# A streaming-encoder trunk: the first norm's factors spread over the partitions by TensorE, and residual loads, additions and operand preparation moved in the down-projection

## The chip, the cores and the metric

The kernel runs on one core of one Trainium2 chip. The time is device microseconds of that core, the median of several runs. The profile is one execution of the program, taken by the hardware profiler; its times are microseconds from the start of its span.

## What is computed

Two layers on 1024 tokens of width 1024, float32. Layer 0 mixes tokens by differential attention, layer 1 by latent attention. Behind each stands a gated MLP with a causal convolution; its last step is the down-projection. Cut to what the change touches:

```python
def rms_norm(x, g):
    xf = x.astype(jnp.float32)
    y = xf * lax.rsqrt(jnp.mean(xf * xf, axis=-1, keepdims=True) + NORM_EPS)
    return (y * g.astype(jnp.float32)).astype(x.dtype)

h = rms_norm(x, attn_norm_g[i])          # g: one factor per feature
x = x + diff_attention(h, ...)           # layer 0; mla_attention in layer 1
h = rms_norm(x, ffn_norm_g[i])
x = x + (jax.nn.silu(g) * val) @ w_down  # conv_ffn: 2816 x 1024
...
return rms_norm(x, final_norm_g)
```

## The kernel before

Every large product is done in three: each operand is split into a high part, rounded to fp32r (`hi`, L127, on ScalarE as a rule), and a low part, the rest (`lo`, L130, on VectorE as a rule), and `mm3` (L119 to L121) sums high x low, high x high and low x high in PSUM. The core's memory is cut by hand into places: 14 of 8 KB per partition (`s0` to `s13`), 16 of 4 KB (`u`), 14 of 2 KB (`h`). PSUM has two double banks (`S`, from `big`) and four single ones: three with the tag `b`, one with the tag `u`. A tile that takes a bank waits until the last reader of the tile before it there is done.

In regions marked `manual_schedule`, the instructions of the engines named stand in the order in which the code issues them; elsewhere a scheduler with simulated times sets the order. Each engine works its queue strictly in that order, SP's queue (most DMA issues) too. A DMA issued from SP is held, besides its data, until the one eight places before it has landed.

*The prologue* (`diff_attention`, from L412). Token tiles of 128 x 1024 are loaded one by one. For each: `squares` (L157, ScalarE) sums the squares, `root` (L164 on VectorE, L167 on GpSimd) makes the reciprocal root, `norm` (L422, VectorE) multiplies the tile by the root and by the factors `g`, `turn` (L430) transposes it in eight 128x128 pieces into two `b` banks, `high` and `low` split it. `g` is the vector `attn_norm_g[0]`, loaded by `gain` (L193) as 128 copies of 4 KB: one DMA of 512 KB into `s11`, second in SP's queue. Between the tiles stand the splits of the first head's weights (`w_high`, `w_low`) and its first products on half a token block (`piece`, 24 matmuls of 128x256 each). The order is written out by hand for TensorE, VectorE and ScalarE.

*The down-projection* (`down`, L1261). The inner dimension of 22 blocks is taken in two parts. Blocks 0 and 1 are done plainly: for each of the eight token tiles, 12 matmuls of 128x512 into two banks, `y`, then two additions of `y` to the residual `X` (L1429, VectorE). The token tiles alternate between two `b` banks and a `b` and the `u` bank, so a tile waits for the additions two tiles before it. The other 20 blocks are done by a Strassen-like scheme on ten pairs of blocks: two groups of five pairs, each with seven products (M5, M1, M3, M2 and so on), each product over its five pairs j. One step is one product of one pair: 12 matmuls. A step's operands are sums of quarter blocks (`sums`, L1293, VectorE, where there are any), their high parts (`high`, ScalarE) and low parts (`low`, VectorE). `advance` issues them ahead of use: in one call the sums of two steps later, the high parts of the next step, and the low parts of the current one, all counted by `at.low`. It is called after the plain token tiles 4, 6 and 7, and after each step. The quarter blocks are loaded by `fetch` (L1283), the residual by `fetch_x` (L1339), 1 MB for two token tiles. Products are added to the residual by `evict` (L1449). While the plain tiles run, VectorE also finishes the up-projection's last block (L1113, L1119), whose result goes to DRAM (L1122, from ScalarE's queue) and comes back as a block of the fifth pair.

*Attention of layer 1* (`MlaStep`) is ordered by the scheduler: scores into `S` banks (L119 to L121), exponentials on ScalarE (L2013), transposes of the probabilities (L252), products with the values (L2033, L2034), and the next heads' projections (`b` banks).

## Time and profile before

| | us |
|---|---|
| median of 3 runs | 2403.01 (2402.82 to 2404.68) |
| the profiled execution | 2402.48 |
| its span | 2400.7 |
| busy: TensorE, VectorE, ScalarE, GpSimd | 2345.5, 1947.9, 1290.0, 612.4 |
| prologue and first projections, 0 to 45: TensorE busy | 33.1 |
| opening of the down-projection, layer 0, 990 to 1020 | 28.1 of 30 |
| the same, layer 1, 2189 to 2207 | 14.6 of 18 |
| last stretch of layer 0 and latent projections, 1300 to 1341 | 33.7 of 41 |

The rows of the timeline give start and length of an instruction (us), its engine, its line in the program, the operation with what it writes and reads, and in brackets how long the engine was idle before it and what released it. SPq and ACTq are the engines' instruction queues, where DMAs are issued. A matmul's length holds its way through the array; the pace is the distance from one start to the next.

### The profile page before, as it was taken

What the parts mean: (1) busy time and instruction counts of PE and PEld (TensorE: products, weight loads), DVE (VectorE), ACT (ScalarE), POOL (GpSimd) and SP (SyncE); (2) the same over time, 40 slices, a digit from 0 to 9 for tenths busy, and PEclk for the clock granted to TensorE, in tenths of its full rate; (3) what the DMA queues carried; (4) which work ended last, traced back from release to release, by engine and by line L of the source; (5) the groups of instructions that cost most, each with busy time, mean ns of one, the idle gap of its engine ahead of it and who ended that gap; (6) DMA issues with size and microseconds to landing.
All of it is one profiled execution on the core that took longest, in us unless ns stands there. A gap on an engine that the chain in (4) does not pass through costs nothing.

```text
span 2400.7 us, 32598 instructions
## 1 busy us (share of the span) xinstructions
PE 2345.5 (98%) x11936; PEld 1993.4 (83%) x11936; DVE 1947.9 (81%) x3180; ACT 1290.0 (54%) x2366; POOL 612.4 (26%) x484
## 2 busy tenths in 40 slices
PE   7999999999999999999999899999999999999998
PEld 7888888888888888788898789988888888887886
DVE  6888888858888888899864788886488888888997
ACT  5677777745444444444445777775354444443443
POOL 3555555424000000000132666664320000000001
PEclk9999999999999999999999999999999999999999
DMA  3011111333222222642221111123322222227502
GB/s 154 33 43 36 36 47 56 110 101 115 79 89 87 79 79 88 230 168 91 82 97 57 61 40 40 41 88 113 112 73 89 87 79 79 88 79 280 176 1 79
DMA packets 95792, 213.91 MB, mean 89 GB/s; under 512 B 8720, under 2 KB 33936, under 8 KB 95632
## 3 DMA queue, kind: packets, MB, share of 16 engines
q1 hardware_dynamic: 86448, 184.04, 23.1%
q10 hardware_dynamic: 9184, 27.79, 3.1%
q8 instruction: 94, 1.54, 0.3%
q14 instruction: 66, 0.54, 0.1%
HBM read 159.37 MB, written 52.43 MB: 88 GB/s over the span
## 4 chain that ended last, share of the span: by engine, by line
PE 85%; DVE 6%; DMA 3%; ACT 3%; POOL 2%; issue 2%; SPq 0%; POOLq 0%; DVEq 0%; ACTq 0%
PE S L119 13%; PE S L121 13%; PE S L120 13%; PE b L119 8%; PE b L120 8%; PE b L121 8%; PE u L119 4%; PE u L121 4%; PE u L120 4%; PE b L252 2%; PE u L2034 1%; PE u L2033 1%; PE S L1878 1%; PE S L1877 1%; DMA u<-g_d 1%
## 5 line engine op out<-in xcount | busy, mean ns | idle before, releaser
L167 POOL TENSOR_TENSOR st<-st,mhalf 128x1 f32<-128x1 f32 x56 | 36.1, 645 | 1312.7 <-DVE st L164 1304.9
L119 PE MATMUL S<-s,u 128*128 128x512 f32 (+1 forms) x800 | 302.1, 378 | 1.9 <-DVE s L130 1.9
L121 PE MATMUL S<-s,u 128*128 128x512 f32 (+1 forms) x800 | 301.2, 377 | 1.6 <-DVE u L130 0.8
L120 PE MATMUL S<-s,u 128*128 128x512 f32 (+1 forms) x800 | 301.0, 376 | 0.0
L127 ACT CAST u<-h 128x512 fp32r<-128x512 f32 (+2 forms) x242 | 145.5, 619 | 273.1 <-DVE h L1056 272.1
L119 PE MATMUL b<-s,u 128*128 128x512 f32 x588 | 230.7, 392 | 0.9 <-DVE u L130 0.4
L121 PE MATMUL b<-s,u 128*128 128x512 f32 x588 | 229.0, 390 | 0.0
L120 PE MATMUL b<-s,u 128*128 128x512 f32 x588 | 229.0, 389 | 0.0
L1113 DVE SCALAR_TENSOR_TENSOR u<-u,conv,u 128x1023 f32<-128x1023 f32 (+1 forms) x176 | 224.9, 1278 | 0.8 <-ACT u L1109 0.7
L149 POOL TENSOR_TENSOR u<-u,st 128x512 f32<-128x512 f32 (+7 forms) x160 | 172.1, 1085 | 171.5 <-DVE st L2019 104.7
L127 ACT CAST s<-u 128x512 fp32r<-128x512 f32 (+3 forms) x230 | 145.0, 665 | 99.2 <-PE u L121 35.4
L130 DVE TENSOR_TENSOR u<-b,u 128x512 fp32r<-128x512 f32 (+1 forms) x256 | 159.0, 632 | 21.6 <-ACT u L127 19.0
L119 PEld LDWEIGHTS S<-s,u 128*128 128x128 f32 x800 | 150.5, 188 | 30.2 <-DVE s L130 2.5
L121 PEld LDWEIGHTS S<-s,u 128*128 128x128 f32 x800 | 150.5, 188 | 29.5 <-DVE u L130 1.0
L120 PEld LDWEIGHTS S<-s,u 128*128 128x128 f32 x800 | 150.5, 188 | 27.3
L127 ACT CAST u<-b 128x512 fp32r<-128x512 f32 (+1 forms) x256 | 134.7, 546 | 69.2 <-PE b L1924 39.4
L119 PE MATMUL u<-s,s 128*128 128x512 f32 (+1 forms) x408 | 163.6, 401 | 1.9 <-DVE s L130 0.9
L121 PE MATMUL u<-s,s 128*128 128x512 f32 (+1 forms) x408 | 159.0, 390 | 0.0
L120 PE MATMUL u<-s,s 128*128 128x512 f32 (+1 forms) x408 | 158.8, 389 | 0.0
L1116 ACT ACTIVATE u<-u 128x1024 f32<-128x1024 f32 x44 | 46.7, 1062 | 187.4 <-DVE u L1113 187.4
L130 DVE TENSOR_TENSOR s<-u,s 128x512 fp32r<-128x512 f32 (+2 forms) x204 | 139.1, 714 | 9.2 <-ACT s L127 8.9
L130 DVE TENSOR_TENSOR u<-h,u 128x512 fp32r<-128x512 f32 x171 | 117.4, 687 | 32.6 <-ACT u L127 31.5
(280 smaller groups left out, 6527.0 us busy)
## 6 DMA issues: line engine op xcount, KB each, us to landing
u<-in_ffn_up SPq DMA_DIRECT2D x88, 512.0 KB, 3.9
g_d<-u ACTq DMA_DIRECT2D x44, 512.0 KB, 2.6
u<-in_ffn_down SPq DMA_DIRECT2D x66, 256.0 KB, 4.9
u<-g_d SPq DMA_DIRECT2D x62, 256.0 KB, 4.2
s<-in_da_wqkv SPq DMA_DIRECT2D x23, 512.0 KB, 3.6
x_d<-u SPq DMA_DIRECT2D x16, 512.0 KB, 2.9
s<-x_d SPq DMA_DIRECT2D x8, 1024.0 KB, 10.8
u<-o_d SPq DMA_DIRECT2D x24, 256.0 KB, 2.9
```

The source lines that it names most:

```text
L119: mm(out, lh, rl, start=first, stop=False, skip_group_check=onto)
L120: mm(out, lh, rh, start=False, stop=False, skip_group_check=onto)
L121: mm(out, ll, rh, start=False, stop=last, skip_group_check=onto)
L127: self.nc.scalar.copy(out, src)
L130: (eng or self.nc.vector).tensor_sub(out, src, hi.bitcast(F32))
L149: self.nc.gpsimd.tensor_mul(x, x, s.to_broadcast(list(x.shape)))
L167: nc.gpsimd.tensor_tensor(r, s, self.mhalf, ALU.pow)
L252: self.nc.tensor.transpose(ps[:, j * P : (j + 1) * P], probs[t][:, k : k + P], self.ident)
L1113: nc.vector.scalar_tensor_tensor(t[half][:, back:], u[half][:, : S - back], w, t[half][:, back:], ALU.mult, ALU.add)
L1116: nc.scalar.activation(t[0], t[0], AF.Silu)
L1877: nc.tensor.matmul(sc[c][:, b : b + m], ql[c][:, qs], kt[:, c, :m], start=True, stop=False)
L1878: nc.tensor.matmul(sc[c][:, b : b + m], qh[:, c, qs], kt[:, c, :m], start=False, stop=True)
```

## The change

In the prologue, the broadcast load of the factors is gone. The vector is loaded as 8 rows of 128 (4 KB, from ScalarE's queue, before its table load). TensorE transposes it into a column block of 128x8, VectorE copies that to SBUF, and eight transposes, each with one column broadcast over 128 columns as the operand, lay the factors out on all partitions in an `S` bank. The norms of tiles 0 and 1 read them there; ScalarE copies them to `s11` for tiles 2 to 7. Seven matmuls of 128x512 of ones into a `u` bank are added (`spin`), three behind the spread, two behind the transposes of tile 0 and two behind those of tile 1; their operand of ones is written by VectorE at the start. SP's queue is now in the order of the code in the prologue, as is GpSimd's, and the last part of the first value unit is inside the region.

In the down-projection, `advance` issues high, low, sums instead of sums, high, low; the last residual load is issued behind the four blocks of pair 3; and the additions of a token tile are issued in the code behind the next tile's matmuls.

```diff
+    def spin(self, n):
+
+        ps = self.bank("u")
+        for _ in range(n):
+            self.nc.tensor.matmul(ps, self.ones, self.wide, start=True, stop=True)
...
+        self.row = self.at("u13", [8, P])
+        nc.scalar.dma_start(self.row, a["attn_norm_g"][0:1, :].rearrange("o (k p) -> (o k) p", p=P))
         nc.scalar.preload_act_table_set("natural_log_exp_and_others")
...
+        self.wide = self.at("h4", [P, 512], F32R)
+        for j in range(4):
+            nc.vector.tensor_scalar(self.wide[:, j * P : (j + 1) * P], self.ident, 0.0, 1.0, ALU.mult, ALU.add)
...
+        queue = self.tc.manual_schedule(engines={mybir.EngineType.SP})
+        queue.__enter__()
...
-            nc.vector.scalar_tensor_tensor(x[i], x[i], r[i], g, ALU.mult, ALU.mult)
+            nc.vector.scalar_tensor_tensor(x[i], x[i], r[i], g[i], ALU.mult, ALU.mult)
...
         fetch_x(0)
-        g = self.gain("s11", a["attn_norm_g"][0])
         fetch_x(1)
...
+        column = self.bank()
+        nc.tensor.transpose(column[:, 0:KD], self.row, self.ident[0:KD, 0:KD])
+        gains = self.at("h5", [P, KD])
+        nc.vector.tensor_copy(gains, column[:, 0:KD])
+        spread = self.big()
+        for k in range(KD):
+            nc.tensor.transpose(spread[:, k * P : (k + 1) * P], gains[:, k : k + 1].to_broadcast([P, P]), self.ident)
+        g = [spread, spread] + 6 * [self.at("s11", [P, D])]
+        self.spin(3)
         squares(0)
         root(0)
         norm(0)
         squares(1)
+        nc.scalar.copy(g[2], spread)
         root(1)
         turns(0)
+        self.spin(2)
         high(0)
...
         turns(1)
+        self.spin(2)
         high(1)
...
         def advance(to, most=2):

             while at.low <= to and most:
-                sums(at.low + 2)
                 high(at.low + 1)
                 low(at.low)
+                sums(at.low + 2)
...
-        fetch_x(2)
-        for j, names in ((3, ("B12", "A21", "B11", "A22")), (4, ("B12", "A21", "B11", "A22")), (5, ("B12",))):
+        fetch_x(1)
+        for name in ("B12", "A21", "B11", "A22"):
+            fetch(3, name)
+        fetch_x(1)
+        for j, names in ((4, ("B12", "A21", "B11", "A22")), (5, ("B12",))):
...
+            if t:
+                taken(t - 1, *older)
+            older = y
...
-            for b in range(2):
-                x = X[t // 2][:, t % 2, b * 512 : b * 512 + 512]
-                nc.vector.tensor_add(x, x, y[b])
+        taken(NT - 1, *older)
```

What the change moves, first at the start of the program on TensorE. Before, its queue begins with the transposes of token tile 0 (`u_60_156`) and 1 (`u_62_160`) and the first product:

```order
L430 MATMUL b_186<-ident,u_60_156 128x128 x4
L430 MATMUL b_191<-ident,u_60_156 128x128 x4
L430 MATMUL b_205<-ident,u_62_160 128x128 x4
L430 MATMUL b_210<-ident,u_62_160 128x128 x4
L119 MATMUL u_227<-s_49_141,s_73_198 128x256
```

In the change (`h_69_184` is the column block, `h_46_127` the ones, `S_186` the spread factors; L444 is the line of the tokens' transposes now):

```order
L507 MATMUL b_182<-ident,u_45_118 128x8
L512 MATMUL S_186<-ident,h_69_184 128x128 x8
L195 MATMUL u_196<-h_46_127,ones 128x512 x3
L444 MATMUL b_212<-ident,u_62_165 128x128 x4
L444 MATMUL b_217<-ident,u_62_165 128x128 x4
L195 MATMUL u_222<-h_46_127,ones 128x512 x2
L444 MATMUL b_234<-ident,u_63_167 128x128 x4
L444 MATMUL b_239<-ident,u_63_167 128x128 x4
L195 MATMUL u_244<-h_46_127,ones 128x512 x2
L119 MATMUL u_259<-s_51_148,s_80_227 128x256
```

Nine transposes and seven matmuls of ones have come in; the rest stands as it stood.

Second, the opening of the down-projection of layer 0 on VectorE, from the calls of `advance` behind token tile 6 to the last additions. Before (L1293 are sums, L130 low parts, L1429 the additions of tiles 6 and 7):

```order
L1293 TENSOR_TENSOR h_1630_9265<-s_1599_9089,s_1600_9092 128x512
L1293 TENSOR_TENSOR h_1631_9267<-u_1598_9087,s_1599_9089 128x512
L130 TENSOR_TENSOR s_1620_9201<-h_1614_9177,s_1620_9201 128x512
L130 TENSOR_TENSOR s_1620_9201<-h_1615_9179,s_1620_9201 128x512
L1429 TENSOR_TENSOR s_1594_9078<-s_1594_9078,b_9251 128x512
L1429 TENSOR_TENSOR s_1594_9078<-s_1594_9078,b_9252 128x512
L1293 TENSOR_TENSOR h_1635_9290<-u_1623_9224,u_1624_9227 128x512
L1293 TENSOR_TENSOR h_1636_9292<-u_1601_9094,u_1623_9224 128x512
L130 TENSOR_TENSOR s_1632_9269<-h_1618_9197,s_1632_9269 128x512
L130 TENSOR_TENSOR s_1632_9269<-h_1619_9199,s_1632_9269 128x512
L1429 TENSOR_TENSOR s_1594_9078<-s_1594_9078,b_9276 128x512
L1429 TENSOR_TENSOR s_1594_9078<-s_1594_9078,u_9277 128x512
```

In the change the sums are at L1319, the additions at L1433:

```order
L130 TENSOR_TENSOR s_1626_9230<-h_1622_9210,s_1626_9230 128x512
L130 TENSOR_TENSOR s_1626_9230<-h_1623_9212,s_1626_9230 128x512
L1319 TENSOR_TENSOR h_1639_9303<-s_1607_9122,s_1608_9125 128x512
L1319 TENSOR_TENSOR h_1640_9305<-u_1606_9120,s_1607_9122 128x512
L1433 TENSOR_TENSOR s_1605_9118<-s_1605_9118,b_9282 128x512
L1433 TENSOR_TENSOR s_1605_9118<-s_1605_9118,b_9283 128x512
L130 TENSOR_TENSOR s_1638_9298<-h_1627_9235,s_1638_9298 128x512
L130 TENSOR_TENSOR s_1638_9298<-h_1628_9237,s_1638_9298 128x512
L1319 TENSOR_TENSOR h_1644_9328<-u_1631_9257,u_1632_9260 128x512
L1319 TENSOR_TENSOR h_1645_9330<-u_1609_9127,u_1631_9257 128x512
L1433 TENSOR_TENSOR s_1605_9118<-s_1605_9118,b_9307 128x512
L1433 TENSOR_TENSOR s_1605_9118<-s_1605_9118,u_9308 128x512
```

In each call the two low parts have gone ahead of the two sums; the additions stand where they stood. In layer 1 the same rows are exchanged. On SP's queue, the residual's loads (`x_d`) and the blocks of pair 3 before:

```order
L1339 DMA s_1591_9056<-x_d_132 128x2x1024
L1339 DMA s_1593_9076<-x_d_132 128x2x1024
L1339 DMA s_1594_9078<-x_d_132 128x2x1024
L1283 DMA u_1595_9080<-in_ffn_down 128x512
L1283 DMA u_1596_9082<-g_d_135 128x512
L1283 DMA u_1596_9082<-in_ffn_down 128x512
L1283 DMA u_1597_9085<-g_d_135 128x512
```

And in the change:

```order
L1365 DMA s_1599_9089<-x_d_139 128x2x1024
L1365 DMA s_1601_9109<-x_d_139 128x2x1024
L1309 DMA u_1602_9111<-in_ffn_down 128x512
L1309 DMA u_1603_9113<-g_d_142 128x512
L1309 DMA u_1603_9113<-in_ffn_down 128x512
L1309 DMA u_1604_9116<-g_d_142 128x512
L1365 DMA s_1605_9118<-x_d_139 128x2x1024
```

The last residual load has gone behind the four blocks.

Third, TensorE's queue in the attention of layer 1, where the scheduler's order first differs. Before, the scores into `S_12211` stand ahead of three transposes and four products with the values:

```order
L121 MATMUL S_12175<-s_1907_11511,s_1923_11637 128x128
L119 MATMUL S_12211<-s_1907_11511,s_1923_11637 128x256
L120 MATMUL S_12211<-s_1907_11511,s_1923_11637 128x256
L121 MATMUL S_12211<-s_1907_11511,s_1923_11637 128x256
L252 MATMUL b_12040<-ident,u_1981_11941 128x128
L252 MATMUL b_12040<-ident,u_1988_11970 128x128 x2
L2033 MATMUL u_12067<-u_1997_12021,s_1848_11118 128x256
L2034 MATMUL u_12067<-u_1997_12021,s_1848_11118 128x256
L2033 MATMUL u_12067<-u_1997_12021,s_1848_11118 128x256
L2034 MATMUL u_12067<-u_1997_12021,s_1848_11118 128x256
```

In the change (the same scores are `S_12244`; transposes L263, products with the values L2070 and L2071):

```order
L121 MATMUL S_12208<-s_1915_11544,s_1931_11670 128x128
L263 MATMUL b_12073<-ident,u_1989_11974 128x128
L263 MATMUL b_12073<-ident,u_1996_12003 128x128 x2
L2070 MATMUL u_12100<-u_2005_12054,s_1856_11151 128x256
L2071 MATMUL u_12100<-u_2005_12054,s_1856_11151 128x256
L2070 MATMUL u_12100<-u_2005_12054,s_1856_11151 128x256
L2071 MATMUL u_12100<-u_2005_12054,s_1856_11151 128x256
L119 MATMUL S_12244<-s_1915_11544,s_1931_11670 128x256
L120 MATMUL S_12244<-s_1915_11544,s_1931_11670 128x256
L121 MATMUL S_12244<-s_1915_11544,s_1931_11670 128x256
```

The scores have gone behind seven matmuls. From here on some 460 rows of TensorE's queue stand in another order in pieces of this size, the same on ScalarE, VectorE and GpSimd beside them; ahead of it and behind it TensorE's queue is alike but for the rows of the prologue.

## The prediction

> **What bounds the kernel now.** I read the page's busy shares and its chain first, then a table of busy time by stretch of the span (microseconds of the span, then busy time of TensorE, its weight loads, VectorE, ScalarE and GpSimd, granted clock, DMA share, GB/s).

> ```profile
> span 2400.7 us, 32598 instructions
> PE 2345.5 (98%) x11936; PEld 1993.4 (83%) x11936; DVE 1947.9 (81%) x3180; ACT 1290.0 (54%) x2366; POOL 612.4 (26%) x484
> PE 85%; DVE 6%; DMA 3%; ACT 3%; POOL 2%; issue 2%; SPq 0%; POOLq 0%; DVEq 0%; ACTq 0%
> 0.00:14.20 14.20, 3.94 (x16) 3.14 (x16) 6.48 (x10) 7.83 (x13) 4.44 (x15) 1.00 0.82 320
> 990.00:1020.00 30.00, 28.10 (x123) 22.60 (x122) 28.59 (x39) 10.75 (x15) 0.00 (x0) 1.00 0.89 333
> 1027.00:1300.00 273.00, 272.89 (x1374) 236.98 (x1373) 212.31 (x362) 125.37 (x255) 37.37 (x34) 1.00 0.29 95
> 1341.00:1400.00 59.00, 57.87 (x367) 51.63 (x368) 45.63 (x109) 40.61 (x91) 37.69 (x32) 1.00 0.12 36
> 2207.00:2370.00 163.00, 163.00 (x721) 134.97 (x720) 151.58 (x246) 74.48 (x134) 0.00 (x0) 1.00 0.25 81
> ```

> TensorE is busy 98% and is the chain for 85%. What can be won is its idle time, 55 us in all, and matmuls that run below full pace. After each down-projection's opening it has no gap (272.89 of 273 us, 163.00 of 163), so what is won at an opening is carried to the end. The change touches the first 25 us, both openings, and, through the scheduler, the order in the attention of layer 1.

> **The prologue: the norm's factors.** Rows of the timeline are start, length, engine, line, operation, and in brackets the idle time before with its releaser.

> ```profile
> 5.92 0.56 POOL L167 TENSOR_TENSOR st<-st,mhalf 128x1 f32<-128x1 f32 x1 [2.36 <-DVE st L164]
> 6.64 1.28 DVE L422 SCALAR_TENSOR_TENSOR u<-u,st,s 128x1024 f32<-128x1024 f32 x1 [0.87 <-DMA s<-in_attn_norm_g]
> 7.99 1.97 PE L430 MATMUL b<-ident,u 128*128 128x128 f32 x8 [7.99 <-DVE u L422]
> 1.18 5.34 DMA s<-in_attn_norm_g
> g_d<-u ACTq DMA_DIRECT2D x44, 512.0 KB, 2.6
> ```

> The first norm starts at 6.64, put down to the factors' DMA, which landed at 6.52 (1.18 + 5.34). But its other operand, the root, was ready at 5.92 + 0.56 = 6.48. So taking the 512 KB broadcast away brings that norm forward by 0.14 us, no more. The new route: a 4 KB DMA from ScalarE's queue, a transpose, a VectorE copy, eight transposes, in time for 6.48? Eight transposes take 1.97 us. The small DMA is in no row; its neighbours are 2.6 us (issue to landing of a 512 KB store from ScalarE's queue) and 5.34 us (the broadcast). Issued at about 0.8 it lands at 3.4 or at 6.1; with 0.5 us for the first transpose and the copy, and 1.97, the row stands at 5.9 or at 8.6. I take the first, since the store is on the same queue and the broadcast reads 128 times as much: no delay; the far end makes everything after it 2.1 us later. The copy of the row to SBUF on ScalarE costs about what a 128x1024 pass there costs, 1.06 us, and stands behind the second tile's squares. These come earlier, since that tile no longer queues behind the broadcast, so the cast of the first transposed tokens, next on ScalarE, is not held up. The five small VectorE rows ahead of the first norm lie in its wait. The chain through the second norm stays 0.2 us ahead.

> **The prologue: the added products.** Seven products of ones (three, two, two) go to a bank that is overwritten.

> ```profile
> 11.69 1.97 PE L430 MATMUL b<-ident,u 128*128 128x128 f32 x8 [1.74 <-DVE u L422]
> 14.21 0.58 PE L119 MATMUL u<-s,s 128*128 128x256 f32 x1 [0.55 <-DVE s L130]
> 14.59 0.41 PE L120 MATMUL u<-s,s 128*128 128x256 f32 x1
> 14.80 0.41 PE L121 MATMUL u<-s,s 128*128 128x256 f32 x1
> 19.28 0.40 PE L121 MATMUL u<-s,s 128*128 128x256 f32 x1
> 19.49 1.06 PE L430 MATMUL b<-ident,u 128*128 128x128 f32 x8
> 20.30 0.37 PE L119 MATMUL S<-s,s 128*128 128x256 f32 x1
> 23.13 0.28 PE L121 MATMUL S<-s,s 128*128 128x256 f32 x1
> ```

> TensorE starts at half pace: a 128x256 product follows the last after 0.21 us (14.59 to 14.80), and eight transposes take 1.97. The group's last product, at 19.28, is still at that pace; behind it eight transposes take 1.06, and 24 products stand from 20.30 to 23.13, 0.12 apart. The clock column stays 1.00 throughout, so it does not show this gate; the row lengths do. The switch at 19.3 came 5.1 us after the products began at 14.21, the start of uninterrupted work. The gaps before were 1.74 and 0.55.

> At half pace a 128x512 product is 0.43. Three (1.28) lie in the wait for the first norm, two (0.85) in the 1.74 us, and two reach past the 0.55: 0.30 too long, less the 0.2 won before. So products start at 14.28, not 14.21. But TensorE is now uninterrupted from the second tile's transposes on, at 11.45 (11.69 less 0.24). Switching 5.1 us later means 16.55: 10.6 products at 0.21, 13.4 at 0.12, and the group ends at 18.15 instead of 19.4. **That is 1.25 us.** From nothing (the switch stays) to 2.2 (all 24 products fast: 24 x 0.09) are the ends.

> ```profile
> 21.11 1.06 ACT L127 CAST s<-u 128x1024 fp32r<-128x1024 f32 x1
> 23.32 1.22 DVE L130 TENSOR_TENSOR s<-u,s 128x1024 fp32r<-128x1024 f32 x1
> ```

> Does it carry on? The next late thing is the weights' low half: ScalarE's cast at 21.11 waits in order behind the casts of tile 2, which wait for TensorE; VectorE's subtraction at 23.32 follows. Both move with TensorE. I keep 1.25.

> **The down-projection.** First what does not change: the residual additions stand in VectorE's order exactly where they stood, behind the same operations; "one tile later" moved only the text. Two things did move. In each step the low halves now stand ahead of the sums for two products later, and the last residual load stands behind the four blocks of the third pair.

> ```profile
> s<-x_d SPq DMA_DIRECT2D x8, 1024.0 KB, 10.8
> 998.97 0.32 SPq L1283 DMA_DIRECT2D u<-g_d  x1
> 1010.40 1.29 DVE L1293 TENSOR_TENSOR h<-u,u 128x512 f32<-128x512 f32 x2 [0.87 <-DMA u<-g_d]
> 1012.82 1.28 DVE L1429 TENSOR_TENSOR s<-s,b 128x512 f32<-128x512 f32 x2
> 1013.55 0.50 PE L119 MATMUL b<-s,s 128*128 128x512 f32 x1 [1.20 <-DVE s L1429]
> 1023.49 1.29 DVE L1293 TENSOR_TENSOR h<-u,u 128x512 f32<-128x512 f32 x2 [3.46 <-DMA u<-g_d]
> 1024.70 1.29 DVE L130 TENSOR_TENSOR s<-h,s 128x512 fp32r<-128x512 f32 x2
> 1026.05 0.50 PE L119 MATMUL S<-s 128*128 128x512 f32 x1 [1.28 <-DVE s L130]
> 2212.29 0.39 PE L121 MATMUL S<-s 128*128 128x512 f32 x1
> 2213.65 0.39 PE L121 MATMUL S<-s 128*128 128x512 f32 x1
> ```

> Six products take 1.36 us, so a step of twelve takes 2.72. Layer 0 has two waits:
> - 1.20 at 1013.55: token tile 6 needs the bank that the additions of tile 4 (1012.82) free, and these stood behind sums that waited 0.87 for a block issued at 998.97 and landed at 1010.4. (These rows also price the first two norms' reading of their factors from PSUM: two additions take 1.28 with a bank operand and 1.29 without, so nothing.) The load that now goes behind that block is 1 MB: at the stage's 333 GB/s, 3.1 us, more than the 0.87. So the wait goes, and the additions start at 1011.95; TensorE starts 0.73 behind them as before, at 1012.68. The rest of its wait stays, 0.33.
> - 1.28 at 1026.05: the low half at 1024.70 stood behind sums that waited 3.46 for DMA. Now it runs in that idle time. What is late next is the following low half, which still has the waiting sums (1.21) and the last additions (1.20) ahead of it. That DMA waits for VectorE's last up-projection multiply, which also comes 0.87 earlier: sums at 1022.62, low half at 1025.03, TensorE 1.35 behind its start as before, 1026.38, against 1026.05 + 2.72 = 1028.77. **Layer 0 wins 2.4 us.**

> ```profile
> 2189.39 1.29 DVE L1293 TENSOR_TENSOR h<-u,u 128x512 f32<-128x512 f32 x2 [1.19 <-DMA u<-g_d]
> 2203.03 1.29 DVE L1293 TENSOR_TENSOR h<-u,u 128x512 f32<-128x512 f32 x2 [4.01 <-DMA u<-g_d]
> 2205.59 0.50 PE L119 MATMUL S<-s 128*128 128x512 f32 x1 [1.87 <-DVE s L130]
> 2222.45 2.47 DVE L1449 TENSOR_TENSOR s<-s,S 128x512 f32<-128x512 f32 x4
> 2227.48 0.39 PE L119 MATMUL S<-s 128*128 128x512 f32 x1
> ```

> Layer 1 the same way: sums at 2203.03 - 1.19 = 2201.84, TensorE 2.41 + 1.35 later, 2205.60, against 2205.59 + 2.72 = 2208.31. **It wins 2.7.** The cover there is VectorE, busy 93% in the stretch behind. Its evictions end at 2224.92, 2.56 ahead of the products that need them at 2227.48. TensorE comes 2.7 earlier, VectorE 2.4, so 2.2 are left. At the other end, if neither the third pair nor that later DMA came sooner, each layer would win 1.52 (2.39 - 0.87, 2.71 - 1.19).

> **Attention of layer 1.** The scheduler reorders TensorE from 1341 to about 1400, without adding work.

> ```profile
> 1341.21 0.38 PE L119 MATMUL S<-s,s 128*128 128x256 f32 x1 [1.23 <-ACT u L2013]
> 1300.00:1341.00 41.00, 33.69 (x173) 26.67 (x171) 27.17 (x63) 30.96 (x66) 20.27 (x15) 1.00 0.31 94
> ```

> Where it begins, TensorE waited 1.23 us for an exponential; three transposes and four products now stand ahead of that wait and can fill half of it. Behind it scores stand later, and their exponentials with them. In the old order these 59 us have 1.13 idle, so little can be won. I count nothing, between -0.7 and +3.

> **Sum.** The profiled execution took 2402.48, 1.78 more than its span. 2402.48 - 1.25 - 2.4 - 2.7 = 2396.1. The median of the runs, 2403.01, is 0.53 above that execution, so **2396.6** is the forecast, 0.27% below.

> **Rivals.**
> - *The clock switches no sooner.* If transposes do not count as work for the gate, uninterrupted work begins only at the last two added products, 13.4, and the switch comes at 18.5: 0.4 us won, or none. The rows leave this open: with transposes counted, TensorE had worked from 11.69 with a gap of 0.55 only, and still switched 7.6 us later. Time 2397.7. [...] The trace shows only that transposes run at both paces, 1.97 and 1.06 for eight. [...]
> - *Neither block comes sooner.* The DMA is 0.89 busy there. Then the down-projections win 3.0 in all, not 5.1: 2398.7. Against it: the bytes ahead of the third pair fall by 1 MB.
> - *The row comes late*, 2.1 us at the far end: 2398.7.
> - *Slower: the attention's new order.* If the scores that now stand behind other work make TensorE wait as in the 41 us before (7.31 idle, 18%), the 59 us gain 10.5 - 1.1 = 9.4 of idle time: 2406. It ends slower than before from 6.4 on. Against it: VectorE and ScalarE are there 77% and 69% busy.
> - *It does not do what it says*: true of the moved additions, as shown, and priced at nothing.

> **How the numbers follow.** Forecast 0.46, with its own range 2395.2 to 2398.0 (all 24 products fast at the low end); clock no sooner 0.20; blocks no sooner 0.13; late row, or up to 3 us lost in attention, 0.10; both gains larger, below 2395.2, 0.03; slower 0.08. The range 2394.2 to 2400.8 leaves out the slow case and the edges. A measurement here tells about 0.2% from no change, that is below 2398.2: nearly all of the forecast's share (0.44), half of the first rival, a third of the second, the 0.03 and a little of the late row, 0.64 in all. Slower by as much 0.08, the rest 0.28.

> **What would show it.** Right: the first norm at 6.5; rows of 128x256 products turning to 0.12 spacing by 17; the weights' subtraction before 22.4; at the sixth token tile a wait of about 0.3; in the first group of products the wait at the third step gone, with at most 0.6 at the fourth; VectorE's idle before its sums smaller. Wrong: the first norm waiting for a transpose; products at 0.21 until 19; a wait of over 1 us left at the openings; over 2 us of TensorE waiting between 1341 and 1400.

## The result, and the profile after

The changed kernel took 2396.76 us (median of 7 runs, 2394.45 to 2399.01), the kernel before 2404.68 beside it (7 runs, 2402.82 to 2408.06). The ratio is 0.9965, 95% interval [0.9954, 0.9977], so 5.5 to 11 us. The profiled execution took 2396.82, its span 2395.0, that is 5.7 less than before's 2400.7. By the medians the gain is 7.9: the profiled execution of before, 2402.48, is one of its fastest (two of its 40 timed runs in this record were faster), so differences between the two traces show less than the medians do. The forecast of 2396.6 stood on a sum of 6.35 and on a median of before of 2403.0. The time fits; of the terms only some do.

The page of the changed kernel, then its busy time by stretch (columns as in the prediction):

```profile
span 2395.0 us, 32652 instructions
PE 2348.3 (98%) x11952; PEld 1995.3 (83%) x11952; DVE 1947.0 (81%) x3185; ACT 1292.0 (54%) x2367; POOL 613.6 (26%) x484
PE 85%; DVE 6%; ACT 3%; issue 2%; DMA 2%; POOL 2%; SPq 0%; POOLq 0%; DVEq 0%; ACTq 0%
```

```profile
0.00:14.20 14.20, 7.88 (x32) 5.84 (x32) 7.57 (x16) 9.28 (x14) 4.51 (x15) 1.00 0.89 342
990.00:1020.00 30.00, 29.09 (x127) 23.45 (x126) 29.35 (x41) 10.47 (x15) 0.00 (x0) 1.00 0.88 325
1300.00:1341.00 41.00, 35.74 (x181) 29.02 (x180) 28.29 (x71) 32.92 (x71) 23.50 (x18) 0.96 0.35 106
```

The opening of layer 0 has 29.09 busy of 30 (28.10 before), the 41 us ahead of the attention 35.74 (33.69), part of it at half pace (the granted clock there is 0.96). For the rest the two traces were laid on each other: the start of a TensorE instruction in one, less its start in the other. Negative is ahead of before. The first column is the lead at 25 us, the next four what each stage adds to it, the last the lead at the end:

```
execution         at 25   25-595   990-1035   1035-2165   2165-2215   at 2380
the change        -2.27    +1.89      -0.95       -1.87       -2.55     -5.76
prologue_only     -1.57    +1.11      +1.44       -1.46       +0.97     +0.48
down_only         +0.56    +0.05      -1.79       -1.79       -1.59     -4.57
no_ones           -0.54    +1.33      -0.10       -1.34       -2.93     -3.59
load_back         -2.76    +1.73      -1.11       -1.79       -2.83     -6.74
sums_first        -2.53    +2.36      +2.31       -1.04       -0.17     +0.92
more_ones         -2.74    +0.69      -0.93       -2.19       -1.35     -6.53
norm_early        -0.04    +2.40      -0.49       -1.06       -1.80     -1.00
additions_back    -1.18    +3.66      -1.59       -1.51       -3.29     -3.91
low_early         -2.46    +3.29      -2.58       -1.70       -3.41     -6.83
low_early_timed   -2.09    +1.65      -2.56       -1.57       -3.43     -8.01
all_three         -3.18    +2.68      -2.58       -3.17      -3.45     -9.70
```

**Prologue.** TensorE's rows of the changed kernel (L195 the ones, L444 the tokens' transposes), then VectorE's:

```profile
5.42 1.63 PE L195 MATMUL u<-h,ones 128*128 128x512 f32 x3
8.09 1.97 PE L444 MATMUL b<-ident,u 128*128 128x128 f32 x8 [1.05 <-DVE st L164]
9.71 1.20 PE L195 MATMUL u<-h,ones 128*128 128x512 f32 x2
11.80 1.10 PE L444 MATMUL b<-ident,u 128*128 128x128 f32 x8 [0.88 <-DVE u L436]
14.28 0.36 PE L119 MATMUL u<-s,s 128*128 128x256 f32 x1 [0.92 <-DVE s L130]
14.59 0.28 PE L121 MATMUL u<-s,s 128*128 128x256 f32 x1
17.24 1.03 PE L444 MATMUL b<-ident,u 128*128 128x128 f32 x8
```

```profile
6.76 1.28 DVE L436 SCALAR_TENSOR_TENSOR u<-u,st,S 128x1024 f32<-128x1024 f32 x1 [0.75 <-POOL st L167]
9.86 0.69 DVE L130 TENSOR_TENSOR s<-b,s 128x512 fp32r<-128x512 f32 x1 [1.76 <-ACT s L127]
10.47 1.27 DVE L436 SCALAR_TENSOR_TENSOR u<-u,st,S 128x1024 f32<-128x1024 f32 x1
21.04 1.22 DVE L130 TENSOR_TENSOR s<-u,s 128x1024 fp32r<-128x1024 f32 x1
```

The pace turned between the two ones at 9.71 (1.20) and the eight transposes at 11.80 (1.10, not 1.97). So all 24 products ran fast and their group ended at 17.24, before at 19.49. The weights' subtraction stands at 21.04, before at 23.32.

**Where most of that lead was lost again.** A store of a residual tile, the norm that waits for it, and the transposes behind, in the changed kernel; then what else DMA carried from 545 to 548; then the norm before:

```profile
544.41 0.33 SPq L920 DMA_DIRECT2D x_d<-u  x1
...
549.41 1.28 DVE L984 SCALAR_TENSOR_TENSOR u<-u,st,u 128x1024 f32<-128x1024 f32 x1 [2.92 <-DMA x_d<-u]
...
550.75 0.66 PE L881 MATMUL b<-ident,u 128*128 128x128 f32 x4 [1.31 <-DVE u L984]
```

```profile
q8 instruction: 1, 0.02, 3.7%
```

```profile
546.41 0.33 SPq L894 DMA_DIRECT2D x_d<-u  x1
...
549.46 1.28 DVE L958 SCALAR_TENSOR_TENSOR u<-u,st,u 128x1024 f32<-128x1024 f32 x1 [0.95 <-DMA x_d<-u]
```

The norm came 5.0 us behind the store's issue, before 3.05. In between lies one transfer of 16 KB of code (q8, 3.7% of 16 engines for 3 us, that is 1.8 us of one). Before has none in this stretch. The code is TensorE's: q8 has 94 transfers in either trace for 23,872 TensorE instructions before and 23,904 in the change (weight loads counted), one for 254 in the mean; from one to the next TensorE starts 201 to 322 instructions, VectorE and ScalarE 5 to 52.

**The openings** in the changed kernel: the waits at the sixth token tile and at the fourth step, and the way of the block that the sums wait for (store, load, sums); then layer 1:

```profile
1012.21 0.50 PE L119 MATMUL b<-s,s 128*128 128x512 f32 x1 [0.21 <-DVE s L1433]
...
1013.92 0.33 ACTq L1148 DMA_DIRECT2D g_d<-u  x1
...
1018.76 0.32 SPq L1309 DMA_DIRECT2D u<-g_d  x1
...
1023.69 1.29 DVE L1319 TENSOR_TENSOR h<-u,u 128x512 f32<-128x512 f32 x2 [3.80 <-DMA u<-g_d]
...
1027.44 0.50 PE L119 MATMUL S<-s 128*128 128x512 f32 x1 [1.33 <-DVE s L130]
...
2188.06 0.50 PE L119 MATMUL b<-s,s 128*128 128x512 f32 x1 [0.21 <-DVE s L1433]
...
2198.82 1.29 DVE L1319 TENSOR_TENSOR h<-u,u 128x512 f32<-128x512 f32 x2 [3.08 <-DMA u<-g_d]
...
2202.56 0.50 PE L119 MATMUL S<-s 128*128 128x512 f32 x1 [0.56 <-DVE s L130]
```

Both third steps run without a wait. The fourth steps wait 1.33 and 0.56. In layer 0 the sums still start at 1023.69 (before 1023.49).

**Ahead of the attention of layer 1.** Of the 1.87 us won from 1035 to 2165, 1.37 were won ahead of 1330, nearly all of it behind 1315, where every queue still stands as it did before. A store and, behind it on SP's queue, a load of weights; a low half on VectorE; TensorE's wait. Before, then the change, where that wait is gone:

```profile
1306.52 0.36 SPq L1622 DMA_DIRECT2D v_d<-u  x1
1310.42 0.35 SPq L135 DMA_DIRECT2D u<-in_mla_w  x1
...
1318.52 1.79 DVE L130 TENSOR_TENSOR s<-h,s 128x512 fp32r<-128x512 f32 x1
...
1322.80 0.50 PE L119 MATMUL S<-s,s 128*128 128x512 f32 x1 [0.93 <-ACT u L2013]
```

```profile
1305.20 0.36 SPq L1659 DMA_DIRECT2D v_d<-u  x1
1308.39 0.35 SPq L135 DMA_DIRECT2D u<-in_mla_w  x1
...
1316.22 0.69 DVE L130 TENSOR_TENSOR s<-h,s 128x512 fp32r<-128x512 f32 x1
```

In before 16 KB of code came 0.34 us behind the store, which landed 3.9 us after its issue; in the change no code came near it, and it landed in 3.2. The load went out 0.7 sooner behind the store, and VectorE's low half took 0.69, not 1.79. Over the whole span TensorE's waits for the exponentials fell from 7.0 us (8 of them) to 4.5 (5).

### The profile page after: what moved, and what is told of

The parts are those of the page before. It is cut to its first block, busy times and chain, and to the rows that moved or that the text cites. A ratio compares the mean times of both kernels' runs of the same rounds, so it can differ in the third digit from the quotient of the medians.

```text
span 2395.0 us, 32652 instructions
## 1 busy us (share of the span) xinstructions
PE 2348.3 (98%) x11952; PEld 1995.3 (83%) x11952; DVE 1947.0 (81%) x3185; ACT 1292.0 (54%) x2367; POOL 613.6 (26%) x484
## 4 chain that ended last, share of the span: by engine, by line
PE 85%; DVE 6%; ACT 3%; issue 2%; DMA 2%; POOL 2%; SPq 0%; POOLq 0%; DVEq 0%; ACTq 0%
PE S L119 13%; PE S L121 13%; PE S L120 13%; PE b L119 8%; PE b L120 8%; PE b L121 8%; PE u L119 4%; PE u L121 4%; PE u L120 4%; PE b L263 2%; PE u L2071 1%; PE u L2070 1%; PE S L1915 1%; PE S L1914 1%; PE b L1961 1%
## 5 line engine op out<-in xcount | busy, mean ns | idle before, releaser
L167 POOL TENSOR_TENSOR st<-st,mhalf 128x1 f32<-128x1 f32 x56 | 36.2, 647 | 1307.9 <-DVE st L164 1300.0
L119 PE MATMUL S<-s,u 128*128 128x512 f32 (+1 forms) x800 | 302.1, 378 | 2.5 <-DVE s L130 2.1
L121 PE MATMUL S<-s,u 128*128 128x512 f32 (+1 forms) x800 | 301.1, 376 | 0.4 <-DVE u L130 0.4
L120 PE MATMUL S<-s,u 128*128 128x512 f32 (+1 forms) x800 | 301.0, 376 | 0.0
L127 ACT CAST u<-h 128x512 fp32r<-128x512 f32 (+2 forms) x242 | 145.6, 619 | 273.3 <-DVE h L1082 271.6
L119 PE MATMUL b<-s,u 128*128 128x512 f32 x588 | 230.7, 392 | 1.8 <-DVE u L130 1.3
L121 PE MATMUL b<-s,u 128*128 128x512 f32 x588 | 229.0, 389 | 0.0
L120 PE MATMUL b<-s,u 128*128 128x512 f32 x588 | 229.0, 389 | 0.0
L127 ACT CAST s<-u 128x512 fp32r<-128x512 f32 (+3 forms) x230 | 145.4, 665 | 94.7 <-PE u L121 27.1
L119 PEld LDWEIGHTS S<-s,u 128*128 128x128 f32 x800 | 150.5, 188 | 30.9 <-DVE s L130 2.7
L130 DVE TENSOR_TENSOR u<-b,u 128x512 fp32r<-128x512 f32 (+1 forms) x256 | 158.6, 631 | 20.8 <-ACT u L127 18.2
L121 PEld LDWEIGHTS S<-s,u 128*128 128x128 f32 x800 | 150.5, 188 | 28.1 <-DVE u L130 0.6
L120 PEld LDWEIGHTS S<-s,u 128*128 128x128 f32 x800 | 150.5, 188 | 27.4
L127 ACT CAST u<-b 128x512 fp32r<-128x512 f32 (+1 forms) x256 | 134.9, 546 | 71.1 <-PE b L1961 39.7
L119 PE MATMUL u<-s,s 128*128 128x512 f32 (+1 forms) x408 | 162.4, 398 | 2.2 <-DVE s L130 1.3
L121 PE MATMUL u<-s,s 128*128 128x512 f32 (+1 forms) x408 | 157.9, 387 | 0.0
L120 PE MATMUL u<-s,s 128*128 128x512 f32 (+1 forms) x408 | 157.7, 387 | 0.0
L130 DVE TENSOR_TENSOR s<-u,s 128x512 fp32r<-128x512 f32 (+2 forms) x204 | 139.0, 715 | 11.8 <-ACT s L127 11.4
L130 DVE TENSOR_TENSOR u<-h,u 128x512 fp32r<-128x512 f32 x171 | 117.4, 687 | 32.5 <-ACT u L127 31.5
## 6 DMA issues: line engine op xcount, KB each, us to landing
u<-in_ffn_up SPq DMA_DIRECT2D x88, 512.0 KB, 3.8
g_d<-u ACTq DMA_DIRECT2D x44, 512.0 KB, 2.6
s<-in_da_wqkv SPq DMA_DIRECT2D x23, 512.0 KB, 3.6
x_d<-u SPq DMA_DIRECT2D x16, 512.0 KB, 3.0
s<-x_d SPq DMA_DIRECT2D x8, 1024.0 KB, 10.4
```

What stands on the lines that cost most here:

```text
L119: mm(out, lh, rl, start=first, stop=False, skip_group_check=onto)
L120: mm(out, lh, rh, start=False, stop=False, skip_group_check=onto)
L121: mm(out, ll, rh, start=False, stop=last, skip_group_check=onto)
L127: self.nc.scalar.copy(out, src)
L130: (eng or self.nc.vector).tensor_sub(out, src, hi.bitcast(F32))
L167: nc.gpsimd.tensor_tensor(r, s, self.mhalf, ALU.pow)
```

## The experiments

Theory behind the first: the change wins in the prologue, at both openings and in the attention, and loses 1.9 to the late store. Rival: the prediction's account (1.25, 2.4, 0, 2.7). Unless said otherwise an experiment is the changed kernel with the edit shown. Where no ratio is given, it is one execution.

**prologue_only**, the change with `down` as before:

```diff
-                high(at.low + 1)
-                low(at.low)
                 sums(at.low + 2)
+                high(at.low + 1)
+                low(at.low)
...
-            if t:
-                taken(t - 1, *older)
```

(and the last residual load ahead of pair 3.)

> The change's prologue with the down-projection of before. Theory (the prologue saves 2.3 us on TensorE and keeps them; the changed kernel's profiled run lost 1.9 of them at 549 us to one store that happened to land 4.9 us after its issue, not 2.6 to 3.0): the second group of 128x256 products starts at 18.0 and not 20.3; transposes of the normed tiles between 540 and 580 wait under 0.6 us in all for a norm; both waits at each opening of the down-projection are as before (1.2 and 1.3; 1.5 and 1.9). Ratio to before about 0.999. Rival (the late store comes of the earlier start): the wait of 1.3 us at 550 is there again, the lead behind 580 us is 0.4, ratio 0.9998. Where the scheduler orders the attention of layer 1 anew, its waits for exponentials are read apart: 7.0 us before, 4.5 in the change.

Ratio 0.9992 [0.9983, 1.0]. The pace turned only at 15.3:

```profile
14.70 0.58 PE L119 MATMUL u<-s,s 128*128 128x256 f32 x1
15.08 0.38 PE L120 MATMUL u<-s,s 128*128 128x256 f32 x1
15.29 0.28 PE L121 MATMUL u<-s,s 128*128 128x256 f32 x1
```

1.57 were won, 1.11 lost by 595: the late store is there again (4.2 us). It is no chance of one execution, so the theory's word "happened" falls. The openings waited 1.63 and 2.31, 2.40 and 0.33: all four waits are there, as the theory had it, but not in before's sizes. The stretch 1035 to 2165 won 1.46 with before's down-projection, 1.41 of it ahead of 1330: that gain comes with the prologue.

**down_only**, before with the change's `down`:

> The change's down-projection with the prologue of before; the attention of layer 1 stands in the order of the change. Theory: layer 0's opening wins 2.2 us where the store of the last up-projection block lands in 2.7 to 3.0 us (1.1 where it takes 4.8 as in the changed kernel's profiled run), the attention's order wins 2.1 (five waits for exponentials, 4.5 us, in place of eight, 7.0), layer 1's opening 2.5: 6.8 us, ratio 0.9972. The prediction's account: 2.4, 0 and 2.7, ratio 0.9979. Rival for layer 0 (the later residual load always delays that store): its fourth step waits 1.3 us again.

Ratio 0.9977 [0.9968, 0.9986]. The openings won 1.79 and 1.59 (the theory said 2.2 and 2.5); the fourth step of layer 0 waited 0.40, so the rival falls. The stretch with the attention won 1.79, but only 0.25 of it ahead of 1330: there 16 KB of code came 0.37 us behind the store of `v_d`, as in before, the low half took 1.81, and TensorE waited 0.71. The prologue is before's, and so is the residual store's way (3.05). The two ratios multiplied give 0.9969; the change has 0.9965. The attention of layer 1 is ordered anew in both kernels, here as in the change, in prologue_only in a third way. So the kernel with the down-projection's edits alone has most of the gain.

**no_ones**:

```diff
-        self.spin(3)
...
-        self.spin(2)
```

(all three calls, and their operand `wide`.)

> The changed kernel without the seven products of ones and their operand. Theory (the products of ones bring the clock's switch forward): the first group of 128x256 products starts at about 14.0 at a distance of 0.21 us and turns to 0.12 no sooner than 17; the group ends 1 to 2.2 us later than the change's 17.24. Rival (the nine transposes that spread the factors warm TensorE enough): products at 0.12 from their start, nothing lost.

The first group began at 14.23 at half pace and turned here:

```profile
18.03 0.39 PE L121 MATMUL u<-s,s 128*128 128x256 f32 x1
18.24 0.29 PE L119 MATMUL u<-s,s 128*128 128x256 f32 x1
18.37 0.28 PE L120 MATMUL u<-s,s 128*128 128x256 f32 x1
```

The group ended at 18.96, 1.7 behind the change. The spreading transposes alone do not bring the pace. The store was on time (3.03); the 1.33 lost by 595 is a stretch at half pace at 455, 6.8 us long here and 3.4 in before (last section).

**load_back**:

```diff
-        fetch_x(1)
+        fetch_x(2)
         for name in ("B12", "A21", "B11", "A22"):
             fetch(3, name)
-        fetch_x(1)
```

> The changed kernel with the last residual load ahead of the four blocks of pair 3 again. Theory (the load's place is what makes the sums' block come in time): the sixth token tile waits about 1.1 us in layer 0 and 1.4 in layer 1 for its bank again, the sums ahead of it wait for DMA, and the third step still has no wait. Rival (the low halves ahead of the sums do it all): the sixth tile waits 0.2 as in the change, and nothing is lost.

The sixth tile waited 0.33 and 0.19, the third steps not at all. The rival holds: with the low halves first, the load's place does not matter to these waits.

**sums_first**, the first diff's order of the calls alone, the load still behind pair 3:

> The changed kernel with the order of before in the calls of the helper that prepares the steps (sums, high, low), the last residual load still behind pair 3. Theory (the low halves ahead of the sums do it all, as the run with the load put back had no wait of over 0.33 us at the sixth token tile and none at the third step): the third step waits 1.2 to 2.3 us again in both layers, the sixth tile 1.2 to 2.4. Prediction's account (the later load brings the block in time): the sixth tile waits 0.3, only the third step's wait is back.

```profile
1012.42 0.50 PE L119 MATMUL b<-s,s 128*128 128x512 f32 x1 [0.21 <-DVE s L1433]
1026.58 0.50 PE L119 MATMUL S<-s 128*128 128x512 f32 x1 [2.99 <-DVE s L130]
```

The sixth tile waited 0.21 in both layers, the third step 2.99 and 2.93. So either edit is enough for the sixth tile, as the prediction's account had it for the load, and only the low halves' place removes the third step's wait. With the load moved alone, the third step waits longer than in before (1.28, 1.87) and prologue_only (2.31, 0.33).

**more_ones**:

```diff
-        self.spin(3)
+        self.spin(6)
...
-        self.spin(2)
+        self.spin(4)
...
-        self.spin(2)
+        self.spin(3)
```

> The changed kernel with thirteen products of ones (six, four, three) in place of seven (three, two, two). So far TensorE turned to its fast pace at 6.8, 11.3 and 15.3 us in three executions of the same prologue, and at 18.3 to 20.3 in three without the ones. [...] Rival (the switch needs products on normed tokens, or falls anywhere): later than 11. Should the fourteen tokens' transposes be pushed back by the ones, the products start after 14.3.

The pace turned within the six ones from 5.42 to 7.8; products started at 13.82, all fast, the last of the group at 16.64. The rival's "later than 11" did not come. The code came at 543.9, 1.5 us earlier than the change's 545.39; but that was with the store's issue (543.86) and no longer behind it. The norm came 3.3 us behind the store, and 0.69 was lost by 595, not 1.89: how late the store is goes with the code's place.

**additions_back**, the additions written behind their own tile's matmuls:

```diff
-        taken(NT - 1, *older)
+            taken(t, *y)
```

> The changed kernel with the additions of a token tile written in the code ahead of the next tile's matmuls again. Every engine's queue holds the same instructions in the same order as the change's, so this is the change measured once more. Theory (the moved text does nothing): ratio to before 0.996 to 0.998; sixth token tile 0.2 us, no wait at the third step, 0.2 to 2.1 at the fourth; a switch of TensorE's pace anywhere from 6 to 16 us; the store of 544 us late by 1 to 2. Rival (the later additions free a bank later or earlier): the sixth tile's wait is over 0.6.

Ratio 0.9969 [0.9959, 0.998], 2396.51 us beside 2404.13 before. The queues are the change's, so "one tile later" is worth nothing. Here the pace turned at 16.5.

**low_early**, the fourth step's low halves ahead of the sums that wait:

```diff
                 low(at.low)
+                if at.low == 2:
+                    low(3)
                 sums(at.low + 2)
```

(and `low` skips what is done.)

> The changed kernel with the low halves of the fourth step issued ahead of the sums of the fifth and of the last additions. Theory (the fourth step's wait, 0.2 to 2.1 us by execution, is VectorE's: those sums wait 3.1 to 4.6 us for a block that has been stored and loaded again, and the low halves stand behind): no wait of over 0.3 at the fourth step in either layer, a wait of up to 1 at the fifth where the block is late; 0.4 to 1.9 us won over both layers. Rival (the bank of the first group or the high halves hold the step): the wait stays.

```profile
1019.82 2.48 DVE L130 TENSOR_TENSOR s<-h,s 128x512 fp32r<-128x512 f32 x4
1023.93 1.29 DVE L1319 TENSOR_TENSOR h<-u,u 128x512 f32<-128x512 f32 x2 [1.62 <-DMA u<-g_d]
```

VectorE splits both steps while it would wait. From 1020 to 1040 and 2195 to 2220 TensorE does not wait. The openings won 2.58 and 3.41, where the change's `down` won 0.10 to 1.79 and 1.35 to 3.29 over six executions.

> The changed kernel with the fourth step's low halves ahead of the fifth's sums, timed. Theory: its one look had no wait of TensorE between 1020 and 1040 nor between 2195 and 2220, where the change waited 1.33 and 0.56, 1.07 and 0.32, 1.33 and 1.80 in three executions: 1 to 3 us less than the change, ratio to before 0.9955 to 0.997. Rival (what is won there is lost to later waits): ratio as the change's run beside it.

Ratio 0.9962 [0.9948, 0.9975], additions_back beside it 0.9969. The rows, 2.56 and 3.43, are 1.1 to 3.7 us better over both openings than the six executions with the change's `down`; the timing by itself does not tell.

**norm_early**:

```diff
-        parts_low(0, 0)
         norm(1)
+        parts_low(0, 0)
         parts_low(0, 1)
-        squares(2)
         turns(1)
         self.spin(2)
         high(1)
+        squares(2)
```

> The changed kernel with the second tile's norm ahead of the first low half on VectorE, and the third tile's squares behind the second tile's high parts on ScalarE. Theory (with the broadcast gone the second tile's root is ready at 8.5 us, but its norm stands in VectorE's queue behind a low half that waits 1.76 us for ScalarE): the norm starts at 8.7 and not 10.5, the first product at 13.4 to 13.7 and not 14.3, 0.6 to 0.9 us won. Rival (ScalarE's casts or the weights' low half hold the products): the start stays at 14.1 or later.

The norm came at 9.36, but the products at 15.02:

```profile
14.11 0.15 DVE L164 TENSOR_SCALAR st<-st 128x1 f32<-128x1 f32 x1 [1.04 <-ACT u L157]
14.19 1.28 DVE L130 TENSOR_TENSOR s<-b,s 128x512 fp32r<-128x512 f32 x2
...
15.02 0.40 PE L119 MATMUL u<-s,s 128*128 128x256 f32 x1 [2.18 <-ACT s L127]
```

A 0.15 us operation of the third tile's root stood ahead of the low half and waited for the squares that had moved. Behind the 2.18 us of idle (busy 1.24 of the 3.42 us up to 15.18) TensorE ran at half pace again. The stretch from 15 to 19 in this kernel (the granted clock is the last column but two):

```profile
15.00:19.00 4.00, 3.98 (x21) 4.00 (x22) 3.56 (x5) 1.06 (x3) 1.46 (x1) 0.57 0.92 326
```

**all_three**, low_early and norm_early with the root behind too, ones 6, 1, 4:

```diff
         w_low(1)
-        root(2)
         low(1)
+        root(2)
```

> The changed kernel with the early low halves, the second tile's norm ahead of the first low half, the third tile's squares and root behind the second tile's parts, and eleven products of ones (six, one, four). [...] Rival (the idle stretch between the ones and the first product drops the pace, as in the run before, where 2.18 us of idle were followed by 3.4 us at half pace): the first products 0.21 apart, 1 us lost.

2392.05 us (2391.14 to 2394.23), ratio 0.995 [0.9937, 0.9962]: the fastest version here, 4.5 below additions_back beside it, and all five runs below the lowest of that (2394.86).

```profile
10.35 1.26 PE L444 MATMUL b<-ident,u 128*128 128x128 f32 x8 [0.93 <-DVE u L436]
13.37 0.36 PE L119 MATMUL u<-s,s 128*128 128x256 f32 x1 [0.83 <-DVE s L130]
```

Products at 13.37, all fast. Against the change's rows, 0.9 is the prologue's, some 2.5 the openings'. The attention's stretch won 3.17 where the others won 1.0 to 2.2; no half-speed stretch (last section) fell there, as one did in all the others.

## Why the prediction was right, and where not

## What to carry to other kernels

Where a queue is served in order, put what is ready ahead of what waits for a transfer: that order alone won the openings (load_back), and one more step of it (low_early) left no wait at their third to fifth steps. After an engine's input comes earlier, go through the hand-written order again, with the small operations too: the second norm stood at 10.47 and could run at 9.36, and a 0.15 us operation spoiled the first try. Instructions added at the start moved the later loads of code here (all 94 came earlier than in before, by 0.2 to 12.4 us), and one store landed late with it (4.9 us behind its issue, 2.95 in before) and another on time (3.2, 3.9 in before); look for stores near such loads. Give a gain by an earlier switch of the clock as a range (one prologue turned at 6.6 to 16.5 us here), and compare stage by stage over several executions before you trust that a sum came out.

## What the runs showed of the hardware

Behind stretches with much idle time TensorE also fell back to half pace in mid-kernel, for 3.4 us or 6.8. In the change it was busy 0.99 of the 3.41 us ahead of the fall at 455.00 and 1.70 of the 3.44 ahead of that at 1335.64, in before 1.48 of the 3.42 ahead of that at 456.43; 1.39 of 3.40 in before from 1334.60 brought none. The changed kernel behind the waits of 454 to 456:

```profile
454.00:455.00 1.00, 0.33 (x1) 0.30 (x2) 0.00 (x0) 0.98 (x2) 0.92 (x2) 1.00 0.02 8
456.00:458.00 2.00, 2.00 (x9) 1.75 (x8) 1.28 (x3) 1.60 (x3) 0.83 (x1) 0.50 0.00 0
458.00:459.00 1.00, 1.00 (x8) 1.00 (x8) 0.96 (x3) 0.20 (x1) 1.00 (x2) 0.79 0.52 147
```

The last column but two is the granted clock, 0.50 to about 458.4. Every execution has this one: 3.4 us long in before and in six of the table, 6.8 in the other six, which is over 1 us of the scatter in the column 25-595. Another falls within 1329 to 1343 in eleven of twelve (the 0.96 above), none in before and none in all_three; sums_first had one more behind its wait of 2.99, prologue_only one behind its 2.40. By an estimate from these stretches, an idle stretch of 2 to 3 us may so cost 1.7 us (half of 3.4) more than itself.
